# Expert layer on one core: eight more tokens move from the dense path to the gathered path

## The chip, the cores and the metric

The kernel runs on one core of one Trainium2 chip. The metric is device time in microseconds (us) of one launch of the whole program; the time of a kernel is the median of its runs.

The core has five engines that matter here. TensorE (PE in the profile, with its weight loads shown apart as PEld) multiplies; VectorE (DVE) and ScalarE (ACT) do elementwise work; GpSimd (POOL) issues the gathers; SyncE (SP) issues the plain transfers. Sixteen DMA engines carry the bytes of both kinds of transfer. SBUF is the on-chip memory of 128 partitions, PSUM the memory that TensorE writes to.

## The reference, cut to what matters

The program is two transformer blocks over 256 tokens of width 1024. The change touches the last layer alone, an expert layer with 16,384 experts: every token picks 8 x 16 = 128 experts, each with one row of `peer_u` and one of `peer_v`.

```python
def peer(xn, w_pq, subkeys, peer_u, peer_v):      # xn: 256 tokens x 1024
    q = (xt @ w_pq).reshape(T, PEER_HEADS, 2, PEER_QDIM // 2)
    s = jnp.einsum('thpd,hpnd->thpn', q, subkeys)
    top_s, top_i = lax.top_k(s, PEER_TOPK)
    ...                                            # 16 x 16 candidates per head, the best 16 kept
    gate = jax.nn.softmax(best_s, axis=-1)
    def block(args):
        xb, eb, gb = args
        act = jax.nn.gelu(jnp.einsum('thkd,td->thk', peer_u[eb], xb), approximate=False) * gb
        return jnp.einsum('thk,thkd->td', act, peer_v[eb])

x = x + peer(rmsnorm_2(x, g_peer), w_pq, peer_subkeys, peer_u, peer_v)
return rmsnorm_2(x, g_final)
```

## The kernel before

All layers ahead of the expert layer are untouched and take the first 1,000 us or so. The expert layer (`phase_peer`) treats the tokens in two ways at once.

**Dense path, 192 tokens (`TD = T - TS`).** For these tokens all 16,384 experts are computed, in 128 columns of 128 experts. In the **U stage** (the loop over j from L1640 on) column j loads one 128x1024 block of `u` and multiplies its eight 128-wide slices with the transposed tokens, which gives 128 experts x 192 tokens; GELU of it goes to `A[:, j, :]`. Most columns are multiplied in fp32 as they come (L1648, tile `xf`). Where `is_split(j)` holds, the block is split by ScalarE and VectorE into a rounded part `hi` and a rest `lo` (`granule`, L216 and L217), and each slice takes one product of `hi` with 2 x 192 columns and one of `lo` with 192 (L1650, L1651). The routing weights of the dense tokens are laid over `A` by `gates()`: for every token one small fp32 product of two one-hot tables (L1557), made from column `J0 = 75` on, since the tables of the routing stand in the back of `A` until then. `pump` spreads these products over the columns from J0. In the **V stage** column j splits a block of `v` and a column of `A` (`column`), and adds hi and lo products into eight PSUM banks `acc[c]` (`add`, L1701 with 384 columns and L1702 with 192).

**Gathered path, 64 tokens (`TS`).** These are the last 64 tokens. Only their own 128 rows of `u` and `v` are fetched. Each token has two partitions of 64 picks each; `es` holds the row numbers, `gs` the routing weights, `hs` the products, `x2` the tokens themselves. For pick column c one indirect transfer issued by GpSimd (L1474) brings 128 rows of 1024 into one of four `row` tiles; VectorE multiplies and sums them against `x2` (L1459, the u picks), and later scales and adds them into `sacc` (L1464, the v picks). There are 64 + 64 such steps. At the end the lower half of `sacc` is copied over (`low`, L1486) and both halves are added to x.

The order on each engine is fixed when the program is built: a scheduler lays instructions out by priority, and each engine works through its own queue in that order. `Pace` says how many steps of a generator go into how many columns: `rows_early` 33 gather steps over columns 12 to 74, `rows_late` 53 over columns 75 to 127, `rows_v` 48 over the first 112 columns of the V stage; `routes` do the same for the routing. Each gather and each of its VectorE steps is also tied behind the latest matmul (`behind`).

SP's queue carries the loads of `u` and `v` (L1519 and L212), and among them the three small copies of `es` and `gs` (L1424 to L1426) and the copy of `x2` (L1505). In the V stage the loads go to four `raw` tiles, and from column 40 on every other one to a part of `A` that is no longer needed.

After the last column the eight banks are added (L1742, L1743), turned by PE transposes (`turn`, L1728 and L1729), added to x, normalized and written out.

Of the kernel before, what the change touches and what calls it, by code (L numbers as in the profile page):

```python
# [9 lines left out]
F32 = mybir.dt.float32  # L10
# [91 lines left out]
def layout(I):  # L102
# [91 lines left out]
class K:  # L194
# [12 lines left out]

    def granule(self, ap, w=1024, raw=None):
# [4 lines left out]
        hi = self.ring.tile([128, 1024], F32R, name="hi", bufs=3)  # L213
        lo = self.ring.tile([128, 1024], F32R, name="lo", bufs=3)
# [1092 lines left out]
def phase_peer(k, pool, wpool, out):  # L1307
# [5 lines left out]
    TS = 64  # L1313
    TD = T - TS
    S0 = 128 - TS
# [24 lines left out]

    es = wpool.tile([128, 64], I32, name="es", bufs=1)
    gs = wpool.tile([128, 64], F32, name="gs", bufs=1)
    hs = wpool.tile([128, 64], F32, name="hs", bufs=1)
    x2 = wpool.tile([128, D], F32, name="x2", bufs=1)

# [60 lines left out]
    def gather(tt):  # L1406
# [11 lines left out]
        if tt == 1:  # L1418

            own = slice(S0, 128)  # L1420
            e = slot(8, 64).bitcast(I32)
            V.scalar_tensor_tensor(e[own], ri[own, 0:64], 128.0, rj[own, 0:64], op0=OP.mult, op1=OP.add)
            V.scalar_tensor_tensor(es[own], ri[own, 64:128], 128.0, rj[own, 64:128], op0=OP.mult, op1=OP.add)
            nc.sync.dma_start(es[0:S0], e[own])  # L1424
            nc.sync.dma_start(gs[0:S0], bv[own, 0:64])
            nc.sync.dma_start(gs[own], bv[own, 64:128])  # L1426
        ps = k.tp()
# [17 lines left out]
    def behind(i, how):  # L1445
        k.tc.add_manual_dep(i.ins, beat[0].ins.name, mybir.DependencyInfo(how, mybir.DependencyReason.DATA), reason="pace")


    def gathered():
        AHEAD = 3  # L1450
        todo = []
        sacc = None

        def take():
            nonlocal sacc
            kind, c, r = todo.pop(0)
            col = slice(c, c + 1)
            if kind == "u":
                i = V.scalar_tensor_tensor(r, r, 1.0, x2, op0=OP.mult, op1=OP.mult, accum_out=hs[:, col])  # L1459
            elif c == 0:  # L1460
                sacc = wpool.tile([128, D], F32, name="x2", bufs=1)
                i = V.tensor_scalar(sacc, r, hs[:, col], None, op0=OP.mult)
            else:
                i = V.scalar_tensor_tensor(sacc, r, hs[:, col], sacc, op0=OP.mult, op1=OP.add)  # L1464

            behind(i, mybir.DependencyClass.NoSync)
            if (kind, c) == ("u", 63):
# [17 lines left out]
        low = wpool.tile([128, D], F32, name="row", bufs=4)  # L1485
        nc.sync.dma_start(low[S0:128], sacc[0:S0])  # L1486
        x = k.x[S0:128, 1, :]
        V.tensor_tensor(x, x, sacc[S0:128], OP.add)
        yield
        V.tensor_tensor(x, x, low[S0:128], OP.add)  # L1490
        yield

    J0 = 75
    early, late = routing(1), routing(0)
    for c in range(16):
# [3 lines left out]
        if c == 12:  # L1499
# [3 lines left out]
            V.tensor_scalar(xn[1], k.x[:, 1, :], inv[:, 1:2], None, op0=OP.mult)  # L1503
            V.tensor_tensor(x2[S0:128], xn[1][S0:128], gpeer[S0:128], OP.mult)
            nc.sync.dma_start(x2[0:S0], x2[S0:128])  # L1505

# [100 lines left out]
    for c in range(8):  # L1607
        ps = k.tp()
        nc.tensor.transpose(ps[:, 0:128], xn[0][:, c * 128:c * 128 + 128], k.ident)
        nc.tensor.transpose(ps[:, 128:TD], xn[1][0:S0, c * 128:c * 128 + 128], k.ident[0:S0, 0:S0])  # L1610
        col = k.gains[:, GCOL["peer"] + c:GCOL["peer"] + c + 1]
# [105 lines left out]
    last = [column(j) for j in range(128 - LAST, 128)]  # L1717
    oT = A[:, 6:14, :]
    part = A[:, 40:48, :]
# [4 lines left out]
    def turn(c):  # L1724
# [3 lines left out]
        nc.tensor.transpose(tps[0][:, s], oT[:, c, 0:128], k.ident)  # L1728
        nc.tensor.transpose(tps[1][0:S0, s], oT[:, c, 128:TD], k.ident)  # L1729
        if c % 4 == 3:  # L1730
# [82 lines left out]
```

## Time and profile before

| | us |
|---|---|
| median of 3 runs | 1750.54 |
| lowest and highest run | 1750.13, 1755.73 |
| the profiled execution: its own time | 1753.15 |
| the profiled execution: its span, first to last instruction | 1751.4 |
| U stage without gates, 1054.7 to 1253.8 us of the span | 199.1 |
| U stage with gates, 1253.8 to 1437.2 us | 183.4 |
| V stage, 1437.2 to 1739.3 us | 302.1 |
| end, 1739.3 to 1751.4 us | 12.1 |

Times in the profile are counted from the first instruction of the span. L numbers are lines of the kernel before. A row of a timeline gives start, duration, engine, line, operation and tiles; "xN" merges N instructions that follow each other; brackets give how long the engine had been idle and what released it. An fp32 matmul appears as two instructions, the other kind (fp32 data rounded to a shorter form, here called the rounded kind) as one.

### The profile page before, as it was taken

The page shows a single profiled execution, that of the slowest core. Times are in us where ns is not written, and L with a number is a line of the kernel's source. Part 1 is how long each engine was busy: PE and PEld are TensorE (multiplying, and loading weights), DVE is VectorE, ACT ScalarE, POOL GpSimd, SP SyncE. Part 2 cuts the span into 40 slices and gives each one's busy share as a digit, 9 for nine tenths or more (in the row PEclk, how much of TensorE's full clock was granted, in tenths as well). Part 3 has the DMA queues.
Part 4 walks back from the last instruction along what each step waited for, and adds up shares of the span by engine and source line. Part 5 has one row for each costly group of instructions (what it writes and reads, how often), then busy time and mean ns, then how long its engine had stood idle before and what let it go on. Part 6 is the DMA issues. An engine that isn't in the chain of part 4 may idle for free.

```text
span 1751.4 us, 29395 instructions
## 1 busy us (share of the span) xinstructions
PE 1711.7 (98%) x10902; PEld 1572.5 (90%) x10902; DVE 1311.6 (75%) x2562; ACT 997.6 (57%) x2025; POOL 249.5 (14%) x184
## 2 busy tenths in 40 slices
PE   8999999999999999999999999999999999999997
PEld 6888888888888888988878899999999999999996
DVE  6867886678678857754366689888689998888875
ACT  6646554555555547766545543233589885555554
POOL 2000000000000000132000000222334344233300
PEclk9999999999999999999999999999999999999999
DMA  7436556653566666532356456888979889999962
GB/s 244 126 111 186 182 186 189 177 178 104 150 193 193 187 193 195 169 111 73 97 174 212 128 169 192 313 303 303 321 269 323 292 305 365 348 331 333 326 229 70
DMA packets 105360, 374.40 MB, mean 214 GB/s; under 512 B 12384, under 2 KB 14080, under 8 KB 104832
## 3 DMA queue, kind: packets, MB, share of 16 engines
q1 hardware_dynamic: 86080, 303.31, 53.2%
q0 software_dynamic: 19136, 69.21, 11.1%
q8 instruction: 86, 1.41, 0.3%
q14 instruction: 58, 0.48, 0.1%
HBM read 368.20 MB, written 3.15 MB: 212 GB/s over the span
## 4 chain that ended last, share of the span: by engine, by line
PE 77%; DVE 8%; issue 6%; ACT 4%; DMA 4%; POOL 0%; SPq 0%; ACTq 0%; POOLq 0%; DVEq 0%
PE acc L222 10%; PE acc L224 10%; PE acc L223 10%; PE acc L270 9%; PE acc L1648 8%; PE acc L271 5%; PE tp L1701 4%; PE acc L1701 4%; PE acc L1650 3%; DVE lo L217 2%; DMA raw<-in_u 2%; PE tp L1702 2%; PE acc L1702 2%; PE tp L1557 1%; PE tp L1165 1%
## 5 line engine op out<-in xcount | busy, mean ns | idle before, releaser
L217 DVE TENSOR_TENSOR lo<-raw,hi 128x1024 fp32r<-128x1024 f32 (+2 forms) x438 | 535.0, 1222 | 261.7 <-ACT hi L216 258.0
L216 ACT CAST hi<-raw 128x1024 fp32r<-128x1024 f32 (+2 forms) x438 | 455.6, 1040 | 461.0 <-PE acc L224 152.6
L270 PE MATMUL acc<-xa,hi 128*128 128x512 f32 x704 | 246.9, 396 | 0.0
L271 PE MATMUL acc<-xa,lo 128*128 128x256 f32 x704 | 196.4, 279 | 0.0
L222 PE MATMUL acc<-xa,hi 128*128 128x256 f32 x568 | 165.9, 292 | 0.8 <-ACT hi L216 0.8
L224 PE MATMUL acc<-xa,lo 128*128 128x256 f32 x568 | 162.3, 286 | 1.2 <-DVE lo L217 1.2
L223 PE MATMUL acc<-xa,hi 128*128 128x256 f32 x568 | 162.4, 286 | 0.0
L1648 PE MATMUL acc<-xf,raw 128*128 128x192 f32 x864 | 160.8, 330 | 0.7 <-ACT ub L1662 0.7
L270 PEld LDWEIGHTS acc<-xa,hi 128*128 128x128 f32 x704 | 132.2, 188 | 31.6
L1701 PE MATMUL tp<-xa,hi 128*128 128x384 f32 x504 | 153.9, 361 | 1.0 <-ACT hi L216 1.0
L1701 PE MATMUL acc<-xa,hi 128*128 128x384 f32 x504 | 154.0, 362 | 0.0
L1648 PEld LDWEIGHTS acc<-xf,raw 128*128 128x128 f32 x864 | 140.1, 193 | 1.0 <-ACT ub L1662 0.9
L1474 POOL DMA_INDIRECT row<-in_v,es x64 | 110.1, 1720 | 183.7 <-DVE xa L282 91.9
L271 PEld LDWEIGHTS acc<-xa,lo 128*128 128x128 f32 x704 | 132.6, 188 | 0.0
L1702 PE MATMUL tp<-xa,lo 128*128 128x192 f32 x504 | 126.8, 253 | 3.2 <-DVE lo L217 3.0
L1702 PE MATMUL acc<-xa,lo 128*128 128x192 f32 x504 | 127.0, 252 | 0.0
L1474 POOL DMA_INDIRECT row<-in_urow,es x64 | 83.9, 1311 | 275.2 <-PE tp L1379 86.9
L1650 PE MATMUL acc<-xa,hi 128*128 128x384 f32 x368 | 121.9, 383 | 0.0
L222 PEld LDWEIGHTS acc<-xa,hi 128*128 128x128 f32 x568 | 109.4, 193 | 2.8 <-ACT hi L216 1.2
L224 PEld LDWEIGHTS acc<-xa,lo 128*128 128x128 f32 x568 | 109.1, 192 | 2.1 <-DVE lo L217 1.7
L223 PEld LDWEIGHTS acc<-xa,hi 128*128 128x128 f32 x568 | 109.5, 193 | 0.6 <-issue 0.2
L1702 PEld LDWEIGHTS tp<-xa,lo 128*128 128x128 f32 x504 | 96.3, 192 | 4.6 <-DVE lo L217 4.4
(483 smaller groups left out, 3949.1 us busy)
## 6 DMA issues: line engine op xcount, KB each, us to landing
raw<-in_u SPq DMA_DIRECT2D x100, 512.0 KB
raw<-in_v SPq DMA_DIRECT2D x84, 512.0 KB
raw<-in_gate SPq DMA_DIRECT2D x44, 512.0 KB
raw<-in_up SPq DMA_DIRECT2D x44, 512.0 KB
raw<-in_down SPq DMA_DIRECT2D x44, 512.0 KB
A<-in_v SPq DMA_DIRECT2D x44, 512.0 KB
raw<-in_gates SPq DMA_DIRECT2D x16, 512.0 KB
raw<-in_pq SPq DMA_DIRECT2D x16, 512.0 KB
```

Of the source, the lines that this page charges most:

```text
L216: nc.scalar.copy(hi[:, :w], raw[:, :w])
L217: nc.vector.tensor_tensor(lo[:, :w], raw[:, :w], hi.bitcast(F32)[:, :w], OP.subtract)
L222: mm(ps, ah, bl, start=start, stop=False)
L223: mm(ps, ah, bh, start=False, stop=False)
L224: mm(ps, al, bh, start=False, stop=stop)
L270: mm(ps, wh[:, s], act.both[:, k].rearrange("p a t -> p (a t)"), start=k == 0, stop=False)
L271: mm(ps[:, T:2 * T], wl[:, s], ah[:, k, :], start=False, stop=k == kn - 1)
L1474: i = nc.gpsimd.indirect_dma_start(out=r, out_offset=None, in_=table, in_offset=bass.IndirectOffsetOnAxis(ap=es[:, c:c + 1], axis=0))
L1648: beat[0] = mm(ps[:, :TD], wh[:, s], xf[:, c], start=c == 0, stop=c == 7)
L1650: mm(ps[:, :2 * TD], wh[:, s], xs[c], start=c == 0, stop=False)
L1701: mm(acc[c][:, 0:2 * TD], vh[:, s], m, start=j == 0, stop=False)
L1702: beat[0] = mm(acc[c][:, 0:TD], vl[:, s], m[:, 0:TD], start=False, stop=j == 127)
```

## The change

The number of gathered tokens goes from 64 to 72, and the dense ones from 192 to 184. The eight new tokens (numbers 184 to 191) have 16 partitions each (`CX = 128 // TX`), with 8 picks on each partition. So there are 8 more pick columns in `es`, `gs` and `hs` (`COLS = 72`), 8 more gathers of `u` rows and 8 more of `v` rows. The tokens are copied to their 16 partitions by eight small transfers, their picks and weights by sixteen. Their sums over `v` are collected in a second accumulator (`xx`), and at the end, for each of the eight output chunks, one small fp32 product with a 128x8 table of ones (`sel`) adds the 16 partitions of each token and turns the result; a ScalarE copy puts it beside the dense tokens.

`J0` is now worked out from `TD` (72 where it was 75), and the paces change with it.

```diff
+    out["sel"] = np.repeat(np.eye(8, dtype=np.float32), 16, axis=0)
...
     TS = 64
-    TD = T - TS
+    TX = 8
+    CX = 128 // TX
+    COLS = TS + TX
+    TD = T - COLS
...
+            e = slot(9, 128).bitcast(I32)
+            low = slice(S0 - 32, S0)
+            V.scalar_tensor_tensor(e[low], ri[low], 128.0, rj[low], op0=OP.mult, op1=OP.add)
+            for dst, src in ((es, e), (gs, bv)):
+                for t in range(TX):
+                    nc.sync.dma_start(dst[t * CX:t * CX + CX, 64:COLS],
+                                      src[S0 - TX + t:S0 - TX + t + 1, :].rearrange("p (r c) -> p r c", c=TX))
...
             if kind == "u":
-                i = V.scalar_tensor_tensor(r, r, 1.0, x2, op0=OP.mult, op1=OP.mult, accum_out=hs[:, col])
+                i = V.scalar_tensor_tensor(r, r, 1.0, x2[c >= TS], op0=OP.mult, op1=OP.mult, accum_out=hs[:, col])
...
         for kind, table in (("u", urow), ("v", vrow)):
-            for c in range(64):
+            for c in range(COLS):
...
-    J0 = 75
+    J0 = (128 * TD - 16 * T - 2048 - 4096) // TD
...
+            low = slice(S0 - 32, S0)
+            V.tensor_tensor(gpeer[low], xn[1][low], gpeer[low], OP.mult)
+            for t in range(TX):
+                nc.sync.dma_start(x2[1][t * CX:t * CX + CX],
+                                  gpeer[S0 - TX + t:S0 - TX + t + 1, None, :].to_broadcast([1, CX, D]))
...
-    rows_early = Pace(rows, 33, J0 - FIRST)
-    rows_late = Pace(rows, 53, 128 - J0)
-    rows_v = Pace(rows, 48, 112)
+    rows_early = Pace(rows, 36, J0 - FIRST)
+    rows_late = Pace(rows, 61, 128 - J0)
+    rows_v = Pace(rows, 58, 112)
...
     for c in range(8):
         for operands in last:
             add(*operands, c)
+
+        mm(acc[c][:, 2 * TD:2 * TD + TX], spread[0][:, c * 128:c * 128 + 128], sel, start=True, stop=True)
         nc.scalar.copy(part[:, c], acc[c][:, TD:2 * TD])
-        V.tensor_tensor(oT[:, c], acc[c][:, 0:TD], part[:, c], OP.add)
+        V.tensor_tensor(oT[:, c, 0:TD], acc[c][:, 0:TD], part[:, c], OP.add)
+        nc.scalar.copy(oT[:, c, TD:192], acc[c][:, 2 * TD:2 * TD + TX])
```

## Rows read from the trace of the kernel before

**Rows 1.** The page: the span by engine (busy us, share, instructions).
```profile
PE 1711.7 (98%) x10902; PEld 1572.5 (90%) x10902; DVE 1311.6 (75%) x2562; ACT 997.6 (57%) x2025; POOL 249.5 (14%) x184
```
**Rows 2.** Stages: busy us (instructions) of PE, PEld, DVE, ACT, POOL; PEclk, DMA share, GB/s.
```profile
1054.70:1253.80 199.10, 195.97 (x1262) 194.03 (x1262) 164.50 (x520) 67.28 (x150) 40.61 (x33) 1.00 0.82 286
1253.80:1437.20 183.40, 178.29 (x1232) 176.47 (x1231) 165.10 (x324) 160.56 (x485) 68.51 (x52) 0.98 0.86 297
1437.20:1739.30 302.10, 297.47 (x2061) 295.19 (x2059) 243.94 (x310) 164.29 (x256) 84.80 (x44) 0.99 0.83 294
```
**Rows 3.** Instructions by line: count, ns min/median/max, first and last start.
```profile
L1648 PE MATMUL acc<-xf,raw x864: 326/326/527, 1055.6 to 1432.4; 128*128 128x192 f32 x173
L1648 PE MATMUL acc<-xf,hi x224: 326/326/431, 1054.7 to 1421.6; 128*128 128x192 f32 x112
L1648 PE MATMUL acc<-xf,lo x224: 326/326/350, 1056.8 to 1437.2; 128*128 128x192 f32 x112
L1650 PE MATMUL acc<-xa,hi x368: 358/361/478, 1094.4 to 1434.5; 128*128 128x384 f32 x184
```
**Rows 4.** Timeline of PE: fp32 products, of the columns and of the gates.
```profile
1134.73 5.39 PE L1648 MATMUL acc<-xf,raw 128*128 128x192 f32 x32
...
1350.36 0.39 PE L1557 MATMUL tp<-oj,oi 128*128 128x128 f32 x2
1350.58 0.82 PE L1648 MATMUL acc<-xf,hi 128*128 128x192 f32 x4
```
**Rows 5.** Timeline of PE: hi and lo products, V stage, then an earlier layer.
```profile
1600.12 0.36 PE L1701 MATMUL acc<-xa,hi 128*128 128x384 f32 x1
...
1602.97 0.36 PE L1701 MATMUL acc<-xa,hi 128*128 128x384 f32 x1
...
199.62 0.40 PE L270 MATMUL acc<-xa,hi 128*128 128x512 f32 x1
...
204.21 0.40 PE L270 MATMUL acc<-xa,hi 128*128 128x512 f32 x1
```
**Rows 6.** Groups by line on VectorE, U stage with gates: count, busy us, mean ns, idle.
```profile
L1459 DVE SCALAR_TENSOR_TENSOR row<-row,x 128x1024 f32<-128x1024 f32 x34 | 41.4, 1219 | 0.2 <-DMA row<-in_urow,es 0.2
L1531 DVE TENSOR_TENSOR oi<-iota,IT 128x512 f32<-128x512 f32 x46 | 31.4, 683 | 0.0
L1562 DVE TENSOR_TENSOR A<-A,tp 128x324 f32<-128x324 f32 (+44 forms) x48 | 27.2, 566 | 5.2 <-PE tp L1557 4.1 <-PE acc L1651 0.7
```
**Rows 7.** Groups by line on VectorE, V stage.
```profile
L217 DVE TENSOR_TENSOR lo<-raw,hi 128x1024 fp32r<-128x1024 f32 x78 | 95.3, 1222 | 26.7 <-ACT hi L216 26.5
L1464 DVE SCALAR_TENSOR_TENSOR x<-row,hs,x 128x1024 f32<-128x1024 f32 x46 | 58.8, 1279 | 0.0
```
**Rows 8.** Stretches of 20 us and one of 1 us, columns as in rows 2.
```profile
1280.00:1300.00 20.00, 16.89 (x101) 16.59 (x100) 13.38 (x31) 13.89 (x42) 4.22 (x4) 0.83 0.68 243
1300.00:1320.00 20.00, 20.00 (x143) 20.00 (x143) 18.41 (x39) 18.63 (x56) 7.98 (x6) 1.00 0.88 310
1400.00:1420.00 20.00, 20.00 (x144) 19.89 (x143) 20.00 (x35) 18.26 (x57) 7.35 (x7) 1.00 0.92 326
1460.00:1480.00 20.00, 20.00 (x140) 20.00 (x139) 18.40 (x24) 12.09 (x19) 6.90 (x4) 1.00 1.00 376
1685.00:1686.00 1.00, 1.00 (x6) 1.00 (x5) 1.00 (x3) 0.00 (x0) 0.00 (x0) 0.50 0.83 274
```
**Rows 9.** DMA by queue, first 223 us of the V stage (packets, MB, share).
```profile
DMA packets 20682, 75.49 MB, mean 339 GB/s; under 512 B 2296, under 2 KB 2296, under 8 KB 20663
```
**Rows 10.** Timeline of SP's queue, where the picks of the gathered tokens are copied.
```profile
1086.95 0.33 SPq L1519 DMA_DIRECT2D raw<-in_u  x1
1090.28 0.49 SPq L1424 DMA_DIRECT2D es<-A  x1
```
**Rows 11.** Timeline of ScalarE and PE at the longest gap of the U stage.
```profile
1287.89 1.04 ACT L216 CAST hi<-raw 128x1024 fp32r<-128x1024 f32 x1 [3.51 <-DMA raw<-in_u]
...
1289.60 0.80 PE L1557 MATMUL tp<-oj,oi 128*128 128x128 f32 x2 [3.11 <-ACT oj L1542]
```

More of the change, by code (lines that the diff above doesn't have):

```diff
@@ L205, in dump, with granule @@
             self.dumps[name] = tuple(ap.shape)
-    def granule(self, ap, w=1024, raw=None):
+    def granule(self, ap, w=1024, raw=None, parts=None):
         nc = self.nc
@@ L212, in granule @@
         nc.sync.dma_start(raw[:, :w], ap)
-        hi = self.ring.tile([128, 1024], F32R, name="hi", bufs=3)
-        lo = self.ring.tile([128, 1024], F32R, name="lo", bufs=3)
+        hi, lo = parts or [self.ring.tile([128, 1024], F32R, name=n, bufs=3) for n in ("hi", "lo")]
         with self.tc.high_priority(self.lead):
@@ L1339, in phase_peer @@
     IT, JT, GT, NJT, NGT = (wpool.tile([128, TD], F32, name=n, bufs=1) for n in ("IT", "JT", "GT", "NJT", "NGT"))
[L1341 to L1344, printed above, removed]
+    es = wpool.tile([128, COLS], I32, name="es", bufs=1)
+    gs = wpool.tile([128, COLS], F32, name="gs", bufs=1)
+    hs = wpool.tile([128, COLS], F32, name="hs", bufs=1)
+    x2 = [wpool.tile([128, D], F32, name=n, bufs=1) for n in ("x2", "xx")]
+    sel = wpool.tile([128, TX], F32, name="sel", bufs=1)
+    nc.sync.dma_start(sel, I["sel"])
     def broadcast_row(dst, n):
@@ L1422, in gather @@
             V.scalar_tensor_tensor(e[own], ri[own, 0:64], 128.0, rj[own, 0:64], op0=OP.mult, op1=OP.add)
[L1423 to L1426, printed above, removed]
+            V.scalar_tensor_tensor(es[own, 0:64], ri[own, 64:128], 128.0, rj[own, 64:128], op0=OP.mult, op1=OP.add)
+            nc.sync.dma_start(es[0:S0, 0:64], e[own])
+            nc.sync.dma_start(gs[0:S0, 0:64], bv[own, 0:64])
+            nc.sync.dma_start(gs[own, 0:64], bv[own, 64:128])
+            e = slot(9, 128).bitcast(I32)
[5 more added lines that the diff above has]
+                                      src[S0 - TX + t:S0 - TX + t + 1, :].rearrange("p (r c) -> p r c", c=TX))
         ps = k.tp()
@@ L1446, in behind @@
         k.tc.add_manual_dep(i.ins, beat[0].ins.name, mybir.DependencyInfo(how, mybir.DependencyReason.DATA), reason="pace")
+    spread = []
     def gathered():
@@ L1451, in gathered @@
         todo = []
-        sacc = None
+        sacc = [None, None]
         def take():
-            nonlocal sacc
             kind, c, r = todo.pop(0)
@@ L1458, in take @@
             if kind == "u":
-                i = V.scalar_tensor_tensor(r, r, 1.0, x2, op0=OP.mult, op1=OP.mult, accum_out=hs[:, col])
-            elif c == 0:
-                sacc = wpool.tile([128, D], F32, name="x2", bufs=1)
-                i = V.tensor_scalar(sacc, r, hs[:, col], None, op0=OP.mult)
-            else:
-                i = V.scalar_tensor_tensor(sacc, r, hs[:, col], sacc, op0=OP.mult, op1=OP.add)
+                i = V.scalar_tensor_tensor(r, r, 1.0, x2[c >= TS], op0=OP.mult, op1=OP.mult, accum_out=hs[:, col])
+            elif c in (0, TS):
+                sacc[c >= TS] = wpool.tile([128, D], F32, name="xx" if c else "x2", bufs=1)
+                i = V.tensor_scalar(sacc[c >= TS], r, hs[:, col], None, op0=OP.mult)
+            else:
+                a = sacc[c >= TS]
+                i = V.scalar_tensor_tensor(a, r, hs[:, col], a, op0=OP.mult, op1=OP.add)
             behind(i, mybir.DependencyClass.NoSync)
-            if (kind, c) == ("u", 63):
+            if (kind, c) == ("u", COLS - 1):
                 nc.scalar.activation(hs, hs, AF.Gelu)
@@ L1485, in gathered @@
         low = wpool.tile([128, D], F32, name="row", bufs=4)
-        nc.sync.dma_start(low[S0:128], sacc[0:S0])
+        nc.sync.dma_start(low[S0:128], sacc[0][0:S0])
+        spread.append(sacc[1])
         x = k.x[S0:128, 1, :]
-        V.tensor_tensor(x, x, sacc[S0:128], OP.add)
+        V.tensor_tensor(x, x, sacc[0][S0:128], OP.add)
         yield
```

10 lines of the change are left out of this document (5 added, 5 removed).

## The prediction

> **What bounds the kernel now.** I read the page first, then the stages, then single groups. TensorE is busy for 98% of the span, VectorE for 75% [rows 1]. The change touches only what runs after 1,050 us, so the stages count: in the U stage without gates, the U stage with gates and the V stage TensorE is busy 195.97 of 199.1, 178.29 of 183.4 and 297.47 of 302.1 us, at a granted clock of 0.98 to 1.00 of full speed [rows 2]. So it sets the end in all three. Next behind it stand, with gates, VectorE (165.1 us, 90%) and the DMA engines (0.86 of their time, 297 GB/s), and in the V stage the DMA engines again (0.83 over the whole, and near the top while rows are still gathered) [rows 2]. The change takes work from TensorE and gives it to exactly these two. The question is how much of the gain they let through.
>
> **What TensorE loses.** Three terms.
>
> *fp32 columns.* 864 + 224 + 224 = 1312 instructions [rows 3], two for each matmul: 82 columns of 8 matmuls. A run of 32 takes 5.39 us, so with the last one's own 0.33 us the spacing is 5.06 / 31 = 163 ns at 192 columns; two gate instructions at 128 columns take 1350.58 - 1350.36 = 0.22 us, 110 ns each [rows 4]. The slope is 53 / 64 = 0.83 ns per column, so eight columns less save 6.65 ns each: 1312 x 6.65 = **8.7 us**.
>
> *Hi and lo products.* A pair with 384 + 192 columns takes (1602.97 - 1600.12) / 10 = 285 ns, a pair with 512 + 256 in an earlier layer (204.21 - 199.62) / 13 = 353 ns [rows 5]. That is 0.354 ns per column, so 16 + 8 columns less save 8.5 ns a pair. There are 368 pairs in the U stage [rows 3] and 128 x 8 = 1024 in the V stage: 1392 x 8.5 = **11.8 us**. Bounds: half of the fp32 slope, 0.415 ns, for all 24 columns gives 13.9 us; if only the 16 columns of the long product count and the short one is already held by something else, 6.6 ns and 9.2 us. I take the slope of the pairs themselves.
> [...] The rows lie between the two rules: 0.354 is under 0.415 but above the 0.277 that two thirds of the columns would leave.
>
> *Gates.* Eight tokens less, 0.22 us each [rows 4]: **1.8 us**.
>
> Together 22.3 us, between 19.7 and 24.4.
>
> **What is added on the path.** The eight small products at the end are fp32 with 8 columns, which no row shows. At most each of their 16 instructions costs what one of 128 columns costs, 0.11 us [rows 4], 1.8 us in all; at least nothing, if they fall into waits of the end. The last columns run back to back until the eighth chunk, so I take the upper end, and 0.2 us for the small ScalarE copies: **2.0 us**.
>
> **What is added beside it, and what it may cost.**
>
> *24 small transfers on SP's queue.* One such issue takes 0.49 us [rows 10], so 24 make some 12 us of SP. Eight (the tokens) come at the start of the U stage, sixteen (picks and weights) near 1,090 us. There SP stood idle from 1087.3 to 1090.28 before the copy of the picks [rows 10], with every later load of `u` queued behind it; now 16 x 0.5 = 8 us more stand there. Loads that are already in flight cover most of it; what is late next is the load behind the copies, then its column. Between 0 and 8 us; I take **2**: eight issues in a row are about 4 us, one and a half columns of 16 x 0.163 = 2.6 us, and the stage lost only 3.1 us to gaps altogether [rows 2], so its loads run ahead by more than one column. The new VectorE steps there (one multiplication of the tokens, one small step for the picks) are under 2 us and lie beside matmuls.
>
> *U stage with gates.* It now has 56 columns instead of 53. TensorE's work before is 178.29 us less what the clock took (0.02 x 183.4 = 3.7), 174.6. Three more columns add two fp32 ones of 16 x 0.163 and one split one of 8 x 0.285, 7.5; the cuts here are 34 x 16 x 6.65 ns = 3.6, 22 x 8 x 8.5 ns = 1.5, and 1.8 for the gates: 175.2 us. VectorE before is 165.1 [rows 2]. It gets 61 row steps instead of 52, 9 x 1.22 = 11.0, and about 2.7 for the other work of three columns; it loses two each of the table steps, 2 x (0.683 + 0.566) = 2.5 [rows 6]. That is 176.3: a tie. Already between 1400 and 1420 us VectorE has no idle time [rows 8]. The DMA engines: a load and a gather are each 128 rows of 1024 fp32, 0.524 MB, so 56 x (1 + 61/56) x 0.524 = 61.3 MB; in 179 us that is 342 GB/s, where the stage now moves 297 and its 1400 to 1420 stretch 326 at a share of 0.92 [rows 2, 8]. Three resources near full at once delay each other, and the cover of a late VectorE step or load is gone. On top of the gaps that are there now I take **4 us**; bounds 0 and 9 (half as much again as one gap like that at 1290 us, priced below).
>
> *V stage.* The 58 steps in 112 columns give 0.524 x (1 + 58/112) = 0.796 MB a column until the gathers end after some 91 columns; at 8 x 276.5 ns = 2.21 us a column that is 360 GB/s. The first 223 us moved 339 on average, and 376 between 1460 and 1480 at a share of 1.00 [rows 8, 9]. If 339 were all that can be had, a column would take 2.35 us, 0.137 more, 12.5 us over 91 columns; if 376, nothing. I take **3 us**, nearer to 376, since the mean is close to what the kernel now asks for: 0.524 x (1 + 48/112) = 0.749 MB in 8 x 285 ns = 2.28 us, 329 GB/s.
> [...] VectorE does not bind here: 243.94 of 302.1 us [rows 2] plus four more row steps of 1.28 us [rows 7].
>
> **Sum.** 22.3 - 2.0 - 2 - 4 - 3 = 11.3 us less. Against the profiled execution (its span 1751.4, its own time 1753.15) that is 1741.9. The median of the runs is 1750.54, 2.6 us lower, and the measured time will be a median: **1739 us**, 0.6% less.
>
> **The rivals.**
> (a) *All of it arrives.* VectorE and DMA fit as they do now; only the end costs: 22.3 - 2.0 = 20.3, 1730 us. For it: the stages before lose only 5 us to gaps at shares of 0.86 and 0.90. Against it: the tie above. 0.17.
> (b) *The DMA engines become the bound.* 339 GB/s in the V stage (12.5 us) and 326 with gates: 61.3 MB / 326 = 188 us where TensorE needs 175.2 plus gaps, some 6 us beyond them. 22.3 - 2 - 2 - 12.5 - 6 = 0, 1751 us. For it: shares of 0.92 and 1.00 now [rows 8]. Against it: 376 GB/s was reached. 0.17.
> (c) *Late loads stop ScalarE, and so the gates (the other side).* At 1287.89 ScalarE had waited 3.51 us for a load of `u`; the one-hot tables queued behind, and PE stood for 3.11 us [rows 11]. [...] For it: 15% more bytes per us in that stage. Against it: the tiles run several columns ahead, and the loads with gates share a longer column. 0.12.
> The forecast with 1733 to 1745 holds 0.54.
>
> **How the numbers follow.** A difference of 0.3%, 5 us, is about what a measurement of this kernel can tell from no change (the runs before lie within 5.6 us). Faster by more: forecast and (a), 0.71. The same: (b), 0.17. Slower: (c), 0.12. The likeliest case's own range is 1733 to 1745. The range reaches down to 1728 (all arrives, with the upper bounds of the pairs) and up to 1755, which takes in (b) and leaves out most of (c).
>
> **What would show it.** In the profile after: L1648's instructions at about 319 ns and a spacing of 156; pairs at 276 ns; 184 gates; the U stage with gates from column 72 with VectorE busy for 95% and more, DMA at 340 GB/s; the V stage at 2.21 us a column and its first 200 us above 350 GB/s. Wrong would be: pairs still at 285 ns (the gain falls to 10.5 us before any loss); PE idle behind ScalarE or a load more than twice with gates (c); a PE gap near 1,090 us of more than 2 us (SP); V columns at 2.3 us with DMA at a share of 1.0 (b).

## The result, and the profile after

The changed kernel takes 1765.09 us (median of 5 runs, 1762.0 to 1766.88) against 1750.54: a ratio of 1.0086, 95% interval 1.0064 to 1.0108. It is slower by 0.9%, where 0.6% faster was forecast. The profiled execution took 1762.0 us, its span 1760.2, 8.8 us more than before. It is the fastest of the five, and the profiled one before was slower than its median, so the stages below account for 8.8 of the 14.6 us between the medians.

The span by engine on the page, and the three stages of the changed kernel (U without gates, U with gates, V; columns as in [rows 2]):

```profile
PE 1705.1 (97%) x10902; PEld 1561.0 (89%) x10902; DVE 1325.7 (75%) x2585; ACT 992.1 (56%) x2022; POOL 246.4 (14%) x200
...
1053.10:1258.40 205.30, 189.93 (x1216) 186.89 (x1216) 166.06 (x527) 63.77 (x146) 42.92 (x36) 0.97 0.84 279
1258.40:1443.20 184.80, 178.79 (x1265) 174.74 (x1263) 172.19 (x336) 158.81 (x479) 81.50 (x60) 1.00 0.92 327
1443.20:1748.00 304.80, 294.86 (x2074) 291.40 (x2073) 249.88 (x315) 164.01 (x261) 66.48 (x49) 0.99 0.84 301
```

TensorE has less to do (1705.1 against 1711.7 us [rows 1]) and yet the kernel ends later. The first stage has three columns fewer and takes 6.2 us more. TensorE is idle there for 15.4 us, against 3.1 before [rows 2], and the mean granted clock fell to 0.97. The stage with gates, which the prediction watched most, is in order. Set against the prediction's own sum, cut into stages (three columns less in the first stage, 7.5 us, one each of the terms for columns and pairs, and the losses where the prediction put them):

| us | forecast | measured | difference |
|---|---|---|---|
| start of the U stage | 1054.7 | 1053.1 | -1.6 |
| U without gates: 199.1 - 7.5 - 6.7 + 2 | 186.9 | 205.3 | **+18.4** |
| U with gates: 183.4 + 0.6 + 4 | 188.0 | 184.8 | -3.2 |
| V: 302.1 - 8.7 + 3 | 296.4 | 304.8 | **+8.4** |
| end: 12.1 + 2 | 14.1 | 12.2 | -1.9 |
| span | 1740.1 | 1760.2 | +20.1 |

**The start of the U stage.** SP's queue and TensorE in the changed kernel, then three stretches of 4 us there and the one behind the first long gap:

```profile
1052.27 11.98 SPq L1524 DMA_DIRECT2D xx<-row  x8
1064.34 2.32 SPq L1539 DMA_DIRECT2D raw<-in_u  x1
...
1072.24 8.02 PE L1668 MATMUL acc<-xf,raw 128*128 128x184 f32 x31 [4.40 <-DMA raw<-in_u]
...
1054.00:1058.00 4.00, 2.92 (x17) 2.28 (x17) 4.00 (x10) 1.85 (x7) 0.00 (x0) 1.00 0.96 28
1058.00:1062.00 4.00, 4.00 (x30) 4.00 (x29) 3.85 (x21) 1.95 (x4) 0.00 (x0) 1.00 0.91 28
1062.00:1066.00 4.00, 4.00 (x27) 4.00 (x26) 4.00 (x25) 0.65 (x2) 0.00 (x0) 1.00 0.95 44
...
1072.20:1076.20 4.00, 3.96 (x13) 3.99 (x14) 4.00 (x22) 0.00 (x0) 0.00 (x0) 0.50 0.77 293
```

The eight copies of the tokens hold SP for 12 us, 1.5 us each, not the 0.49 of the prediction's row [rows 10]. And they do more than hold SP: the DMA engines are busy at a share of 0.91 to 0.96 and move 28 GB/s. Each copy of 64 KB reads one SBUF partition sixteen times. The median copy takes 8.4 us to land. The load behind them starts at 1064.34, and TensorE waits 4.40 us for it. Behind that gap the granted clock is 0.50 for 4 us. Why these copies move so little at that share no run here shows.

The sixteen copies of picks and weights come later on SP:

```profile
1096.99 4.39 SPq L1438 DMA_DIRECT2D es<-A  x7
1101.43 5.06 SPq L1438 DMA_DIRECT2D gs<-A  x8
1106.53 0.58 SPq L1539 DMA_DIRECT2D lo<-in_u  x1
```

**The middle of it.** Both kernels at the same time of the stage, first the kernel before, then the changed one (SP's queue, then TensorE):

```profile
1148.71 4.20 SPq L212 DMA_DIRECT2D raw<-in_u  x2
1153.01 0.96 SPq L1519 DMA_DIRECT2D raw<-in_u  x2
...
1159.45 5.39 PE L1648 MATMUL acc<-xf,raw 128*128 128x192 f32 x32
```

```profile
1145.33 7.55 SPq L213 DMA_DIRECT2D raw<-in_u  x2
1152.99 0.85 SPq L1539 DMA_DIRECT2D raw<-in_u  x2
...
1157.57 0.25 PE L1671 MATMUL acc<-xa,lo 128*128 128x184 f32 x1
1160.41 6.79 PE L1668 MATMUL acc<-xf,raw 128*128 128x184 f32 x32 [2.60 <-DMA raw<-in_u]
```

Two unsplit columns are loaded at 1153 in both. Before, they run 6.44 us later and are there. In the changed kernel TensorE is ready 4.8 us after the issue, and the load needs 7.3. Ahead of it in SP's queue stand two loads of split columns, which took 7.55 us to go out, 4.20 before. What these two waited for, by the waits of SP's queue (us in total, times, longest), in the changed kernel and then in the one before:

```profile
SPq L213 <- DVE ub L1683: 7.1, 1, 7.1
SPq L213 <- DVE lo L217: 5.6, 1, 5.6
...
SPq L212 <- DVE ub L1663: 6.2, 1, 6.2
SPq L212 <- DVE lo L217: 3.4, 1, 3.4
```

Both stood for VectorE, which reads their tiles in its split (L217). So the late load did not wait for its own tile there; it stood in the queue behind loads that did wait. The chain that ends this stage shows the same all along: steps "DMA raw<-in_u" make 22.0% of it, against 5.4% before. Some of its pieces:

```profile
1108.12 8.47 DMA raw<-in_u
...
1125.68 11.30 DMA raw<-in_u
...
1152.99 7.29 DMA raw<-in_u
1160.41 6.79 PE acc L1668 x32
...
1192.77 6.22 DMA raw<-in_u
```

**What the 18.4 us are.** 10.2 us are idle time: 15.4 us, against 3.1 before and the 2 that the prediction allowed. 8.2 us are busy time: 189.93 us, where 195.97 - 7.5 - 6.7 = 181.8 was forecast. A later kernel, few_lead below, does the same 1,216 instructions in 182.52 us at a clock of 1.00, so most of this second part is the lower clock behind the gaps. The idle time by what ended it (us in total, times, longest):

```profile
PE acc L1668 <- DMA raw<-in_u: 8.9, 4, 4.4
PE acc L1668 <- DVE ub L1683: 3.6, 2, 2.1
```

8.9 us ended on loads of `u`, against 0.5 us in the kernel before. 3.6 us ended on VectorE's add of the two parts of a split column (L1683), against 1.5 before.

**The V stage.** One gap stands out. VectorE, SP and TensorE of the changed kernel, then VectorE of the kernel before at the same add:

```profile
1650.71 0.34 DVE L282 TENSOR_TENSOR xa<-A,xa 128x184 fp32r<-128x184 f32 x1
1658.05 1.22 DVE L1505 TENSOR_TENSOR x<-x,row 64x1024 f32<-64x1024 f32 x1 [7.01 <-DMA row<-x]
...
1649.67 0.51 SPq L1500 DMA_DIRECT2D row<-x  x1
...
1660.58 0.52 PE L1722 MATMUL tp<-xa,lo 128*128 128x184 f32 x1 [5.56 <-DVE lo L217]
...
1681.22 1.22 DVE L1490 TENSOR_TENSOR x<-x,row 64x1024 f32<-64x1024 f32 x1 [2.75 <-DMA row<-x]
```

When the old sums are done, their lower half is copied (L1500), and VectorE's queue has the add of this copy (L1505) as its next entry. VectorE stands 7.0 us, with the splits of the next columns behind it, and TensorE 5.6; from 1660.5 to 1664.5 the granted clock is 0.50. The same add was there before too (L1490); VectorE stood 2.75 us for it, and TensorE 2.49.

**What the pairs are worth.** TensorE's timeline in the V stage, and the fp32 products with gates by count and ns (min, median, max):

```profile
1600.66 0.35 PE L1721 MATMUL acc<-xa,hi 128*128 128x368 f32 x1
...
1603.46 0.36 PE L1721 MATMUL tp<-xa,hi 128*128 128x368 f32 x1
...
L1668 PE MATMUL acc<-xf,raw x352: 319/319/347, 1264.4 to 1438.4; 128*128 128x184 f32 x176
```

Ten pairs in 2.80 us are 280 ns each, against 285 [rows 5]. Over the longest undisturbed rows of the V stage (405 pairs here, 540 before) they are 279.8 and 284.5 ns. The fp32 instruction takes 319 ns instead of 326, as forecast.

### The profile page after: what moved, and what is told of

Read it like the earlier page. It is cut to its first block, busy times and chain, and to the rows that moved or that the text cites. A ratio compares the mean times of both kernels' runs of the same rounds, so it can differ in the third digit from the quotient of the medians.

```text
span 1760.2 us, 29485 instructions
## 1 busy us (share of the span) xinstructions
PE 1705.1 (97%) x10902; PEld 1561.0 (89%) x10902; DVE 1325.7 (75%) x2585; ACT 992.1 (56%) x2022; POOL 246.4 (14%) x200
## 3 DMA queue, kind: packets, MB, share of 16 engines
q0 software_dynamic: 21440, 77.60, 12.2%
## 4 chain that ended last, share of the span: by engine, by line
PE 68%; DVE 11%; issue 8%; DMA 7%; ACT 4%; SPq 1%; POOL 0%; ACTq 0%; POOLq 0%; DVEq 0%
PE acc L222 10%; PE acc L224 10%; PE acc L223 10%; PE acc L270 9%; PE acc L1668 5%; PE acc L271 5%; DMA raw<-in_u 4%; PE acc L1721 3%; PE tp L1721 3%; DVE lo L217 3%; DMA raw<-in_v 2%; ACT hi L216 2%; PE acc L1670 1%; PE tp L1165 1%; PE tp L1722 1%
## 5 line engine op out<-in xcount | busy, mean ns | idle before, releaser
L217 DVE TENSOR_TENSOR lo<-raw,hi 128x1024 fp32r<-128x1024 f32 (+2 forms) x438 | 534.4, 1221 | 255.0 <-ACT hi L216 251.4
L1668 PE MATMUL acc<-xf,raw 128*128 128x184 f32 x864 | 158.6, 329 | 8.9 <-DMA raw<-in_u 8.9
L1721 PE MATMUL tp<-xa,hi 128*128 128x368 f32 x504 | 152.1, 358 | 1.0 <-ACT hi L216 1.0
L1721 PE MATMUL acc<-xa,hi 128*128 128x368 f32 x504 | 151.3, 358 | 0.0
L1722 PE MATMUL tp<-xa,lo 128*128 128x184 f32 x504 | 126.8, 252 | 9.0 <-DVE lo L217 8.7
L1488 POOL DMA_INDIRECT row<-in_urow,es x72 | 92.0, 1278 | 269.7 <-PE tp L1384 93.2
L1722 PE MATMUL acc<-xa,lo 128*128 128x184 f32 x504 | 125.6, 249 | 0.0
L1488 POOL DMA_INDIRECT row<-in_v,es x72 | 98.9, 1373 | 182.3 <-PE acc L1722 50.8
L1670 PE MATMUL acc<-xa,hi 128*128 128x368 f32 x368 | 119.6, 380 | 0.0
```

The lines of the kernel that those rows point to most:

```text
L1488: i = nc.gpsimd.indirect_dma_start(out=r, out_offset=None, in_=table, in_offset=bass.IndirectOffsetOnAxis(ap=es[:, c:c + 1], axis=0))
L1668: beat[0] = mm(ps[:, :TD], wh[:, s], xf[:, c], start=c == 0, stop=c == 7)
L1670: mm(ps[:, :2 * TD], wh[:, s], xs[c], start=c == 0, stop=False)
L1721: mm(acc[c][:, 0:2 * TD], vh[:, s], m, start=j == 0, stop=False)
L1722: beat[0] = mm(acc[c][:, 0:TD], vl[:, s], m[:, 0:TD], start=False, stop=j == 127)
```

## The experiments

Ratios are to the kernel before on the same chip, in brackets their 95% intervals. U is the length of the U stage without gates, "idle" TensorE's gaps of 0.15 us and more in it, both from the profiled execution; the changed kernel has 1.0086, U 205.3, idle 15.3, and the one before U 199.3, idle 3.1. Executions of one kernel differ by some 10 us in the whole, so a few us of U in one execution say little by themselves; the ratios are the measure. The diffs are cut to the lines that matter, and the paces of the V stage were set to fit.

| run | ratio | U | idle |
|---|---|---|---|
| xx_pool | 1.0112 [1.0084, 1.0140] | 213.5 | 22.9 |
| xx_dram | 1.0074 [1.0048, 1.0099] | 204.3 | 16.7 |
| picks_pool | 1.0063 [1.0037, 1.0088] | 204.6 | 14.4 |
| before_xx | 1.0033 [1.0015, 1.0050] | 213.4 | 11.5 |
| both_dram | 1.0054 [1.0034, 1.0074] | 199.8 | 13.1 |
| both_late | 1.0023 [1.0004, 1.0042] | 199.9 | 11.5 |
| before_late | 0.9986 [0.9969, 1.0004] | 199.5 | 3.5 |
| before_pace | 1.0035 [1.0019, 1.0052] | 208 | 9.8 |
| before_rows | 1.0012 [0.9993, 1.0031] | 201.4 | 4.6 |
| before_routes | 1.0003 [0.9988, 1.0017] | 200.6 | 4.0 |
| few_rows | 0.9953 [0.9936, 0.9969] | 196.2 | 9.9 |
| few_split | 1.0063 [1.0038, 1.0089] | 214.3 | 19.6 |
| after_few | 1.0060 [1.0041, 1.0079] | 199.4 | 12.3 |
| before_few | 1.0000 [0.9986, 1.0015] | 201.3 | 3.9 |
| few_ahead2 | 1.0114 [1.0094, 1.0134] | 193.5 | 9.0 |
| few_lead3 | 1.0048 [1.0028, 1.0069] | 188.7 | 4.4 |
| after_lead | 1.0031 [1.0019, 1.0043] | 200.4 | 11.8 |
| few_lead | **0.9928** [0.9915, 0.9941] | 187.0 | 4.5 |

### The copies

Five kernels ask what the 24 copies cost: as issues in SP's queue, or as traffic.

**xx_pool**: the eight token copies go to GpSimd's queue.

```diff
-                nc.sync.dma_start(x2[1][t * CX:t * CX + CX],
+                nc.gpsimd.dma_start(x2[1][t * CX:t * CX + CX],
```

> The changed kernel with its eight token copies issued by GpSimd, whose queue is idle there, instead of SP. Theory A (the copies hold up the loads of u that stand behind them in SP's queue): the 4.4 us gap of PE at 1,072 us and the 3 us that the half clock behind it costs go away, 1765 becomes about 1758. Theory B (the copies hold the DMA engines themselves, which show a share of 0.8 to 1.0 at 25 GB/s between 1054 and 1068 us): the loads are issued earlier but land no earlier, 1762 to 1767. Theory C (the denser pace of gathers and routing costs the time, the copies do not matter): 1763 to 1767.

It got no better: 1770.83 us, with an interval that overlaps that of the changed kernel. With SP free, the first loads still did not arrive, now that the copies ran beside them:

```profile
1076.96 7.34 PE L1668 MATMUL acc<-xf,raw 128*128 128x184 f32 x32 [10.03 <-DMA raw<-in_u]
```

**xx_dram**: the tokens go to DRAM in one transfer and come back in one.

```diff
+            nc.sync.dma_start(xd, gpeer[S0 - TX:S0])
+            nc.sync.dma_start(x2[1], xd[:, None, :].to_broadcast([TX, CX, D]))
```

> The changed kernel with the eight token copies replaced by one write of the 8 tokens to DRAM and one read that spreads each over its 16 partitions, both on SP. Theory A: two issues instead of eight, 10 us of SP's queue less, about 1758. Theory B: no 16 transfers read one SBUF partition any more, the DMA engines move loads at their usual rate, about 1758, and the share between 1054 and 1068 us no longer stands near 1 at 25 GB/s. Theory C: 1763 to 1767.

The gap at 1072 shrank from 4.40 to 1.39 us. With xx_pool this points to the traffic more than to the issuing, but not to the traffic alone: with no small copies left (both_dram below) a gap of 2.97 us stands at the same place, and with all of them left it is gone in after_lead. The later gaps stayed or grew (2.17 us at 1113, 2.53 at 1159, 2.08 at 1233), and of the whole, 1764.08 us, nothing certain was won.

**picks_pool**: the sixteen copies of picks and weights go to GpSimd's queue.

```diff
-                    nc.sync.dma_start(dst[t * CX:t * CX + CX, 64:COLS],
+                    nc.gpsimd.dma_start(dst[t * CX:t * CX + CX, 64:COLS],
```

> The changed kernel with its sixteen copies of picks and weights issued by GpSimd instead of SP. Theory A: 9.5 us of SP's queue go away at 1,097 to 1,106 us and with them the gaps of 1.56 and 1.72 us behind it and some low clock, 1757 to 1761. Theory B: these copies are tiny and do not hold the engines, so what they cost is SP's time too, 1757 to 1761. Theory C: 1763 to 1767.

1762.13 us; the interval overlaps that of the changed kernel. The gap at 1072 stayed, 4.29 us.

**before_xx**: the kernel before, with the multiplication of the tokens and the eight copies into a row tile that nobody reads.

```diff
+            xx = wpool.tile([128, D], F32, name="row", bufs=4)
+            for t in range(8):
+                nc.sync.dma_start(xx[t * 16:t * 16 + 16],
+                                  gpeer[S0 - 8 + t:S0 - 8 + t + 1, None, :].to_broadcast([1, 16, D]))
```

> The kernel before, with the multiplication of the 32 token rows and the eight token copies added on SP, into a tile that nobody reads. Theories A and B: the same gap as in the changed kernel, 7 us slower than before, about 1757. Theory C: as before, 1748 to 1753.

The copies (with the small multiplication) cost the kernel before 0.33%, some 6 us, where the prediction had 2 for all 24. (Its profiled execution, 1765.41 us, was far from its median of 1755.31, so its U in the table says little.)

**both_dram**: all 24 copies replaced by three transfers to DRAM and three back, these at column 20 in the program's order (the scheduler put that of the tokens at 1057.60).

```diff
+        if j == 20:
+            nc.sync.dma_start(x2[1], xd[:, None, :].to_broadcast([TX, CX, D]))
+            nc.sync.dma_start(es[:, 64:COLS], ed.rearrange("t (p r) -> (t p) r", r=TX))
+            nc.sync.dma_start(gs[:, 64:COLS], gd.rearrange("t (p r) -> (t p) r", r=TX))
```

> The changed kernel with all 24 small transfers replaced: the 8 tokens, their picks and their weights are written to DRAM with one transfer each, and read back spread over the partitions with one transfer each, issued at column 20 (they are needed from column 60 on). Theory A+B (the copies cost SP's queue and the DMA engines' time; only the place and the form of the 24 transfers matter): PE's idle time in the U stage without gates falls from 15 us to 5, the stage from 205 to 187-190 us, the whole to 1748-1752. Theory C (the denser pace of gathers and routing in the U stage): the stage stays above 198 us, the whole at 1758 or more.

The stage falls by 5.5 us to 199.8, the whole to 1758.62. These are the signs of theory C, not of A+B: the copies are about a third of what the stage lost (18.4 us), and 13.1 us of idle time remain without them.

### The late add

**both_late** is both_dram with the add of the low sums eight gather steps behind their copy (and the pace of the V stage adapted); **before_late** does it to the kernel before, four steps behind.

```diff
-        yield
-        V.tensor_tensor(x, x, low[S0:128], OP.add)
+        for _ in range(9):
+            yield
+        behind(V.tensor_tensor(x, x, low[S0:128], OP.add), mybir.DependencyClass.NoSync)
```

> As both_dram, and the second addition of the sums (the one that needs the copy of the lower half) is tied 8 gather steps, some 15 columns, behind the issue of that copy. Theory D (in the V stage VectorE stands 7 us in its queue for this copy, PE 5.6 us behind it and then at half clock): the gap at 1,660 us goes away, 6 to 8 us less than both_dram, 1741-1745 if A+B hold too. Rival to D (the DMA engines are full in this stretch, and the loads of v would be late there anyway): no more than 2 us less than both_dram.

> The kernel before with the addition of the lower half's sums tied 4 gather steps behind the issue of its copy. Theory D: the gap of 2.5 us at 1,684 us and the low clock behind it go away, 4 us less than before, 1744-1747. Rival: as before, 1748-1752.

In both_late the gap is gone, the V stage falls from 302.9 us to 298.6 (first to last product), the ratio from 1.0054 to 1.0023; the two intervals overlap a little, and the pace of the V stage changed with it. The medians, 1758.62 and 1752.10 us, differ by 6.5 us, as theory D had it. In the kernel before V falls from 301.7 to 301.1 and the ratio's interval holds 1, where 4 us were expected. The wait is the same code in both; the changed kernel pays more for it.

### The pace and VectorE's load

The change also moved the paces: 36 gather steps over 60 columns (33 over 63 before), and the routing over three columns fewer.

```diff
-    routes = [Pace(early, 16, FIRST), Pace(late, 29, J0 - 4 - FIRST)]
+    routes = [Pace(early, 16, FIRST), Pace(late, 29, J0 - 7 - FIRST)]
-    rows_early = Pace(rows, 33, J0 - FIRST)
+    rows_early = Pace(rows, 36, J0 - 3 - FIRST)
```

**before_pace** makes both edits in the kernel before, **before_rows** only the gather steps, **before_routes** only the routing.

> The kernel before with the paces of the changed one in the columns before the gates, nothing else of it: 36 gather steps and 29 routing steps laid out over 60 and 56 columns instead of 33 over 63 and 29 over 59. Theory C: PE's idle time in the U stage without gates grows from 3 us to 8 or more, the whole is 5 to 10 us slower than before, 1754-1760. Theories A and B: as before, 1747-1752.

> The kernel before with the gather steps alone at the changed kernel's early pace (36 over 60 columns instead of 33 over 63), routing as before. Theory C1 (three more gathers and their VectorE steps in the stage cost the time): 4 to 7 us slower than before, as before_pace. Theory C2 (the routing steps squeezed into fewer columns cost it): as before, within 2 us.

> The kernel before with the routing steps alone at the changed kernel's pace (29 over 56 columns instead of 59), gathers as before. Theory C2: 4 to 7 us slower than before. Theory C1: within 2 us.

Both together cost 0.35%, 6 us, with TensorE idle for 9.8 us, as theory C had it; 6.9 us of these ended on loads of `u`. Each alone costs at most 0.12%, inside its interval. So the denser pace costs about as much as the copies, and neither half of it is the cause by itself: the stage of the kernel before stands near an edge.

**few_rows** is both_late with 20 early gather steps, the other sixteen moved to the V stage; **few_split** is both_late with one split column in five before the gates instead of two, which takes about 17 us of VectorE's work out.

```diff
-    rows_early = Pace(rows, 36, J0 - FIRST)
+    rows_early = Pace(rows, 20, J0 - FIRST)
```

```diff
-        return j > FIRST and j % 5 in (1, 3)
+        return j > FIRST and j % 5 in ((1, 3) if j >= J0 else (1,))
```

> both_late with 20 instead of 36 gather steps in the columns before the gates and the rest moved to the V stage (76 steps over 124 columns instead of 66 over 127). Theory E (in the U stage without gates VectorE has too little time per column: its splits and sums come late, SP's loads wait in order for the tiles that these free, PE waits for the loads): 16 x 1.2 us of VectorE work less there, PE's idle time in that stage falls from 11.5 to 5 us and the stage from 200 to 190-194 us; the V stage gets 0.61 gathers a column, 382 GB/s, and may give 2 to 5 us back. The whole 1745-1750. Rival (the idle time there does not hang on VectorE's load): the stage stays at 198-201 us, the whole at 1752 or more.

> both_late with one instead of two split columns in five before the gates (12 fewer): 12 x (1.14 + 0.27) = 17 us of VectorE work less in the U stage without gates, 12 x (2.5 - 2.24) = 3 us of PE work more. Theory E: PE's idle time there falls from 11.5 to 5 us, the stage from 200 to 195-198 us, the whole 1747-1750. Rival: the idle time stays at 10 or more and the stage grows to 202-204 us, the whole 1754-1757.

few_rows is faster than both kernels, 1745.91 us. In few_split the stage grew to 214.3 us with less work for VectorE. This does not refute VectorE's load, since the edit also made twelve more columns unsplit, which take their tiles in another order. SP's queue and TensorE there, then TensorE's waits in both_late and in few_split:

```profile
1231.74 0.33 SPq L1539 DMA_DIRECT2D lo<-in_u  x1
1242.86 0.33 SPq L213 DMA_DIRECT2D raw<-in_u  x1
1243.28 0.86 SPq L1539 DMA_DIRECT2D raw<-in_u  x2
1244.23 0.38 SPq L1539 DMA_DIRECT2D hi<-in_u  x1
...
1247.91 4.21 PE L1668 MATMUL acc<-xf,raw 128*128 128x184 f32 x16 [6.49 <-DMA raw<-in_u]
...
PE acc L1668 <- DVE ub L1683: 3.6, 2, 2.1
PE acc L1668 <- DMA raw<-in_u: 3.5, 2, 2.6
...
PE acc L1668 <- DMA raw<-in_u: 16.1, 4, 6.5
```

SP issues nothing for 11 us and then four loads at once; TensorE waits 6.5 us for one of them. With half the splits TensorE no longer waits for VectorE's add (3.6 us in both_late), but its waits for loads grow from 3.5 to 16.1 us. More unsplit columns had made the loads later, and this led to their tiles.

**after_few** and **before_few** move sixteen and fifteen early gather steps to the V stage, in the changed kernel as it stands and in before_late.

> The changed kernel with 20 instead of 36 gather steps in the U stage without gates, and 74 instead of 58 in the V stage; its 24 copies and the early add of the low sums stay. If the early gather steps cost by themselves (few_rows gained 6 us with them moved), it gains about the same here: some 1759 us, against 1765 for the changed kernel. If that gain came only with the copies and the add mended, the time stays near 1765. Its V stage holds 16 steps more with the early add still in it, so that 2 us of loss there are possible.

> The kernel before, with the add of the low sums tied late as in before_late, and 18 instead of 33 gather steps in the U stage without gates, 67 instead of 52 in the V stage. No eight tokens, no copies. If the early gather steps cost by themselves, it gains 2 to 5 us on before_late (0.9986 of before): a ratio of 0.996 to 0.9975, and then the gain of few_rows is that of the steps and not of the eight tokens. If the steps cost only where the eight tokens stand, the ratio stays at 0.9986 within 0.0015.

The changed kernel takes 1760.02 us, 1.0060 against 1.0086 (the intervals overlap), with U at 199.4; the kernel before gains nothing. So the early gather steps seem to cost only where the stage is short of room; of the changed kernel as it stands this is likely, not certain.

### The lead of the loads

Unsplit columns take their tiles in the order `hi`, `raw2`, `raw`, `lo`, `raw2`, `raw` (`granule_u`). `raw2` has one buffer, so its load has to wait for the column three unsplit turns back, and stands in SP's queue accordingly late. **few_lead3** gives it a second buffer, in few_rows, with the space of the fourth row tile; **few_ahead2** gives up the row tile alone.

```diff
-        AHEAD = 3
+        AHEAD = 2
-                r = wpool.tile([128, D], F32, name="row", bufs=4)
+                r = wpool.tile([128, D], F32, name="row", bufs=3)
-            raw = wpool.tile([128, 1024], F32, name=name, bufs=1)
+            raw = wpool.tile([128, 1024], F32, name=name, bufs=2)
```

> few_rows with three instead of four tiles for gathered rows, and two instead of three gathers under way. It is the base for few_lead3. A gather has one column less to land; if that matters, V columns wait for VectorE and the time rises by 2 to 10 us above few_rows (0.9953 of before); if the gathers have room to spare, it stays within 0.002 of it.

> few_ahead2 with the space of the fourth row tile given to a second buffer of the raw2 tile, so that the load of an unsplit column that goes there can be issued six turns of the rotation ahead instead of three. Theory of the lead (a load that is issued only when the column three turns earlier is done lands too late, 5.5 to 10 us against 5 to 9.5 us): the idle time of TensorE in the U stage without gates falls from about 10 us to 6 or less, 4 us in the whole. Rival (the loads are late because SP's queue stands behind a tile that VectorE or ScalarE must free, or because the DMA engines are full): no change beyond 2 us in the stage or 0.0015 in the whole.

The U stage without gates, few_ahead2, then few_lead3:

```profile
1052.70:1246.20 193.50, 184.41 (x1215) 182.16 (x1215) 149.54 (x496) 64.68 (x146) 23.54 (x20) 0.99 0.75 254
```

```profile
1052.90:1241.60 188.70, 184.21 (x1216) 182.05 (x1216) 149.41 (x496) 64.13 (x146) 22.12 (x20) 0.99 0.75 260
```

The same work on every engine, 4.8 us less time, idle time from 9.0 to 4.4; the ratio from 1.0114 to 1.0048. Some 6 of the 11 us in the whole thus lie outside the stage that the expectation was about. Giving up the row tile, with two instead of three gathers under way, cost 1.6% by itself, more than its expectation allowed: TensorE idles 14.6 us in the stage with gates, where few_rows had 5.2.

**after_lead** is the changed kernel, **few_lead** few_rows with its four row tiles; in both, every second `raw2` load before column 60 goes to a part of `A` that is not in use by then.

```diff
-        if name == "raw2":
+        if name == "raw2" and j < 60 and turns[0] % 6 == 5:
+            raw = A[:, 66:72, :].rearrange("p a t -> p (a t)")[:, 0:1024]
+        elif name == "raw2":
```

> The changed kernel, its 24 copies, paces and early add as they are; only every second load that would go to the single raw2 tile goes, until column 60 of the U stage, to a part of A that nothing uses by then. If the single raw2 tile is what makes the loads late in the changed kernel too, TensorE's idle time in the U stage falls from 15.3 us by 4 to 6 us and the time from 1765 to about 1760 us. If the copies and SP's queue hold the loads there, the stage gains under 2 us and the time stays at 1763 to 1766.

> few_rows (its four row tiles) with the same second place for every second raw2 load until column 60. In few_lead3 the second raw2 buffer took 4.6 us of idle time out of the U stage and 11 us out of the whole. Here the U stage should fall from 196.2 to some 191 us and the time from 0.9953 of before to about 0.992, 1740 us, if the lead is the cause; it stays at 0.995 if what few_lead3 gained hung on its three row tiles.

after_lead takes 1757.79 us, 0.55% less than the changed kernel with nothing else touched; the gap at 1072 is gone, and U falls by 4.9 us. TensorE's waits in its U stage:

```profile
PE acc L1670 <- DVE ub L1685: 9.6, 3, 4.8
PE acc L1670 <- DMA hi<-in_u: 0.2, 1, 0.2
```

The waits for loads fall from 8.9 to 0.2 us. That is the lead's part, and it shows the cause. But the waits for VectorE's add of split columns rise from 3.6 to 9.6 us, so the idle time falls only from 15.3 to 11.8 us, less than the 4 to 6 expected. VectorE is the next limit of this stage; no run took this wait out of the changed kernel by itself.

few_lead takes **1739.02 us** (1737.92 to 1740.31) against 1751.45: the fastest of all. Its U stage without gates beside that of few_rows, few_rows first:

```profile
1053.70:1249.90 196.20, 186.15 (x1215) 183.86 (x1215) 148.56 (x494) 64.60 (x146) 23.06 (x20) 0.98 0.73 251
```

```profile
1053.30:1240.30 187.00, 182.52 (x1216) 180.42 (x1216) 148.34 (x494) 64.01 (x146) 23.07 (x20) 1.00 0.75 261
```

9.2 us less at the same work, and the clock back at 1.00. Where the load stands in SP's queue now, and its column:

```profile
1139.56 0.38 SPq L1541 DMA_DIRECT2D A<-in_u  x1
...
1157.99 2.68 PE L1670 MATMUL acc<-xf,A 128*128 128x184 f32 x16
```

18.4 us lie between issue and column, where the changed kernel had 7.4 with a wait in them. SP still stands just ahead of this load, 8.36 us at two loads of split columns from 1131.11 on; the load now comes so early that this does not matter.

## Why the prediction was wrong

**The step that failed** is the one on SP's queue: "Between 0 and 8 us; I take 2 ... so its loads run ahead by more than one column". The stage came out 18.4 us above the forecast, 10.2 of idle time and 8.2 of busy time, most of it at the lower clock. The step inferred room from the small idle time before. But small gaps don't show how much room there is: before, one load was issued 6.44 us ahead of its column and was there, less than the 7.3 us that the same load took in the changed kernel. Three things were missed:

- the price of a copy: 1.5 us of SP and a share of over 0.9 of the DMA engines, where the issue of another copy, 0.49 us, was taken;
- the denser pace of gathers and routing in this stage, which the prediction put at nothing and which cost the kernel before 6 us (before_pace), as much as the token copies (before_xx);
- that the loads behind them had no lead to spend: with a second place for every other `raw2` load TensorE's waits for loads fell from 8.9 to 0.2 us (after_lead).

From the changed kernel to few_lead the stage falls from 205.3 to 187.0 us: 5.5 us with the copies replaced (both_dram), nothing with the late add, 3.7 with sixteen gather steps moved, 9.2 with the second place. These don't simply add up, since the last edit alone is worth 4.9 in after_lead. That 187.0 meets the forecast's 186.9 is in part luck, since the forecast had those sixteen gather steps in the stage.

**The pairs** were sized wrong: 8.5 ns each, at least 6.6, was forecast. 279.8 instead of 284.5 ns give 4.7, or 6.5 us instead of 11.8 over 1392 pairs. The slope from [rows 5] was taken between two sizes far apart and did not hold for the last 24 columns. The lower bound, 9.2 us with the long product's 16 columns alone, was nearer and still too high.

**The V stage** came out 8.4 us above the forecast, and not where the prediction looked. 2.3 us are idle time (9.9 us against 4.6 before and the 3 allowed), with the one gap of 5.56 us at the add of the low sums. 6.1 us are busy time: 3.9 of it the pairs (1024 x 3.8 ns), about 1 the eight small products, which mostly fall ahead of the end, and the rest is not split up further, the low clock behind that gap among it. both_late took 4.3 us out of the stage. The prediction did not name this add, since the diff does not touch it.

**Right were** the fp32 columns (319 ns; 32 of them in 5.18 us, a spacing of 157 ns for 156 forecast), the cost of the end within its bounds (12.2 us, and about 1 us of small products ahead of it, where 2 were taken in all) and that VectorE and DMA would let the stage with gates through: VectorE busy for 172.19 of 184.8 us, 327 GB/s, idle time 5.9 us against 5.0.

**The rivals.** (c), late loads that stop the gates, did not happen: the longest gap with gates is 1.18 us. The sign that it stood for came, but from the stage before. No run shows the 9 us that bounded the loss of the stage with gates; in its place the runs showed 0.9 us more idle time, where 4 were taken, at a granted clock of 1.00. (b), DMA as the bound in the V stage, is refuted: from 1443 to 1640 us the changed kernel moved 361 GB/s, few_lead from 1425 to 1640 us 375, with no gap of TensorE above 1.4 us in either. (a), all of it arrives, would have been 1730 us with the forecast's pairs; with the measured ones it is 1735.3, and few_lead comes within 4 us of it, though with gather steps and an add that (a) left where they were.

**What stays open.** Why the kernel before passes its own U stage with 3.1 us of idle time on the same single `raw2` tile is only argued: its fp32 columns are 4% longer (32 instructions in 5.39 us [rows 4], against 5.18), and no copies stand in front. The second place was not tried in the kernel before, so how much of few_lead's 0.7% is the eight tokens and how much the lead is not settled. The profiled execution before speaks for the tokens: only 0.5 us of TensorE's waits in that stage ended on loads, so a longer lead had little to take there; and moving gather steps and the add gave the kernel before nothing. Nor was VectorE's add of split columns, which holds TensorE for 9.6 us in after_lead, taken out by itself.

## What to carry to other kernels

A stage with little idle time can still have no room (here 3.1 us, and 9.8 with the denser pace alone): before adding transfers, measure how long ahead of its use each load is issued, against how long it takes to land (4.8 and 7.3 us, where TensorE waited 2.60). In a queue that issues in order look for the loads that stand behind one whose tile is not free yet, as here behind two that took 7.55 us to go out. A tile with one buffer in a rotation can leave its load with no lead, and memory that is written only later in the same phase can hold a second one (waits for loads of 8.9 us fell to 0.2). Price a small copy by a measured one of the same form, not by its bytes (eight of 64 KB held SP for 12 us, at a share of over 0.9 of the DMA engines), and place the consumer of a late copy some steps behind it in its engine's order (the gap of 5.56 us was gone in both_late).

## What the runs showed of the hardware

Eight copies that each read one SBUF partition sixteen times (64 KB) kept the DMA engines busy at a share of 0.91 to 0.96 while moving 28 GB/s (44 with the first load of `u` beside them), took SP 0.6 to 2.4 us each to issue, and 4.8 to 12.3 us to land. With the same tokens by way of DRAM the engines moved far more in the same 4 us (1058 to 1062 us, a share of 0.94 to 0.98): 387 GB/s in both_dram, 224 in xx_dram, loads of `u` included. In the V stage one core moved 375 GB/s over some 200 us (few_lead). After a gap of TensorE of 4.4 us and after one of 5.6 us the granted clock was 0.50 for the next 4 us.
